# Five token tiles, one denominator matmul for two exp tiles, and four squares per norm matmul in an eight-core decoder step

## The chip, the cores and the metric

The kernel runs on all 8 cores of one Trainium2 chip, two dies of four cores, each core with its own share of the batch. The metric is the device time of the slowest core in microseconds (us). An execution comes in a fast state, or in a slow one in which the cores of one die are granted a lower TensorE clock (in the execution of 2127.61 us below, cores 0 to 3 had 0.811 to 0.821 and cores 4 to 7 0.991 to 0.993); all comparisons here are between fast executions. Ratios are computed as the mean time of one kernel's fast runs over the mean of the other's fast runs of the same rounds, so they are not quite the ratio of the medians that are quoted.

Engine names: PE is TensorE (PEld its weight loads), DVE VectorE, ACT ScalarE, POOL GpSimd, SP SyncE.

## The reference, cut to what matters

One layer of a decoder: half-step SwiGLU, a mixer, half-step SwiGLU, final norm. Per core: 2048 prompt tokens and 4 sample rows, width 1024. The mixer has dilated windowed attention (3 groups of 4 heads), a gated recurrence (HGRN2) and attention into 256 memory tokens.

```python
def rmsnorm(x, g):
    y = xf * lax.rsqrt(jnp.mean(xf * xf, axis=-1, keepdims=True) + EPS)   # four norms over D_MODEL
...
# attention group: 128-query blocks, each sees its own key block and the one before it ("back")
s = jnp.einsum('nbqhd,nbkhd->nbhqk', qb, kk) * (Dh ** -0.5)
lse = jax.nn.logsumexp(s, axis=-1); p = jnp.exp(s - lse[..., None])
o = jnp.einsum('nbhqk,nbkhd->nbqhd', p, vv)
...
# the groups are merged with weights proportional to their softmax denominators
# memory attention: softmax over 256 keys (two blocks of 128), 4 heads
```

## The kernel before

The program records operations with their dependencies. A list scheduler inside the kernel file then puts them in order with a fixed price for each operation and emits one in-order stream for each engine. The order on PE is frozen when the kernel is built, from prices. All operations are issued from the same helper, so the profile gives them all line 80, and groups are told apart by tile names: `br` is a ring of 13 bf16 tiles of 512 columns, `fr` a ring of 8 f32 tiles, `wp` weights, `hT` the normed input, `XA`/`XB` x and mixer scratch, `cb` constants (mask, ones), `ps`/`nd`/`hb` the PSUM banks.

```python
# the scheduler's prices (ns)
if eng == ACT:   p.cost = (155 if p.kind == "copy" else 260) + p.n * 0.833
elif eng == DVE: p.cost = 160 + p.n * (0.54 if p.bf else 1.04)
else:            p.cost = 230 + p.n * (0.9 if p.kind in ("tensor_copy", "memset") else 2.05)   # POOL
...
# squares: two chunks of x are squared, added on POOL, and go into one norm matmul
elif c % 2 == 0:
    s = pss[k, 0]; actf(s.t[:, 0:n], xv(k, c), AF.Square, ...)
else:
    actf(s2.t[:, 0:n], xv(k, c), AF.Square, ...)
    tt(POOL, b.t[:, 0:n], s.t[:, 0:n], s2.t[:, 0:n], ALU.add, ...)
    mm(p.t[:, 0:n], ones_n, b.t[:, 0:n], c == 1, c == 7, ...)
...
# q/k projection: four tiles of 512 tokens, then 16 matmuls of 4 columns for the sample rows
for ti, (t0, n) in enumerate(MTG):
    for c in range(8): mm(p.t[:, :], wv[:, a, c, :], hT[:, c, t0:t0 + n], c == 0, c == 7, ...)
...
# attention: exp of scores on ACT, causal mask as a product on DVE,
# then denominators (ones_b) and values block by block
actf(t.t[:, 0:o], p.t[:, 0:o], AF.Exp, [p.d], [t.d], scale=SCALE)
tt(DVE, tv, tv, mv, ALU.mult, [t.d, dm], [t.d])
...
for a in (1, 0):
    for q, (kb, po, oc, w) in enumerate(todo):
        lhs = ones_b if a else vb.t[:, kb, :]
        mm(p.t[:, oc:oc + w], lhs, t.t[:, o_ + po:o_ + po + w], ..., late=300.0)
...
# HGRN gates: three f32 sums of 128x512 per head and 512 tokens, on POOL
tt(POOL, t3.t[:, :], t3.t[:, :], t2.t[:, :], ALU.subtract, ...)
```

`late=300.0` asks the scheduler to place such a matmul 300 ns after its operands are ready by its prices, on top of a fixed 250 ns.

The softmax here doesn't subtract the row's maximum and nothing guards it: scores larger than these inputs give would overflow.

Of the kernel before, what the change touches and what calls it, by code (L numbers as in the profile page):

```python
# [174 lines left out]
class Prog:  # L175
# [7 lines left out]
    WAIT = 1200.0  # L183

# [58 lines left out]
    def schedule(self):  # L243
# [61 lines left out]
        while done < n:  # L305
# [76 lines left out]
            if e == ACT and o["aset"] not in (None, table):  # L382
                cost += self.TABLE
                table = o["aset"]
            o["t0"] = start
            if o["dma"]:
                issue = self.SWISSUE if e == POOL else 60.0
                end = free[e] = start + issue
                if o["pool"] == "bulk":
                    fin = start + 12000.0  # L390
                else:
                    pipe[e] = max(pipe[e], start + issue) + o["nbytes"] / self.DMA_RATE[e]
                    fin = pipe[e] + self.DMA_FIX
            else:
                end = free[e] = start + cost
                fin = end + (self.PEDRAIN if e == PE else 0.0)
# [30 lines left out]
    def emit(self):  # L427
# [50 lines left out]
        with ExitStack() as st:  # L478
# [6 lines left out]
            def run(name):  # L485
                def body(e):
                    b = Bound(e)
                    for o in order[name]:
                        for s, k in o["waits"]:
                            e.wait_ge(sems[s], semval[s][k])  # L490
# [20 lines left out]
MTG = [(0, 512), (512, 512), (1024, 512), (1536, 512)]  # L511
HALF = [(0, 1024), (1024, 1028)]
# [38 lines left out]
def build_nc():  # L551
# [153 lines left out]
    def sq(k, c, late=1000.0, pair=True):  # L705
# [4 lines left out]
        b = P.tile(brp)  # L710
        if not pair:
            actf(b.t[:, 0:n], xv(k, c), AF.Square, [dx[k][c]], [b.d])
            mm(p.t[:, 0:n], ones_n, b.t[:, 0:n], c == 0, c == 7, [b.d, dc], [p.d], late=late)
        elif c % 2 == 0:
# [3 lines left out]
        else:  # L718
            s, s2 = pss[k, 0], P.tile(frp)
            actf(s2.t[:, 0:n], xv(k, c), AF.Square, [dx[k][c]], [s2.d])  # L720
            tt(POOL, b.t[:, 0:n], s.t[:, 0:n], s2.t[:, 0:n], ALU.add, [s.d, s2.d], [b.d])
            mm(p.t[:, 0:n], ones_n, b.t[:, 0:n], c == 1, c == 7, [b.d, dc], [p.d], late=late)
# [171 lines left out]
    def att_proj(s, g, si):  # L894
# [5 lines left out]
        for a in range(2):  # L900
            dst = qk_r[si][a]
            for ti, (t0, n) in enumerate(MTG):
                p = P.tile(psM)
                for c in range(8):
                    mm(p.t[:, :], wv[:, a, c, :], hT[:, c, t0:t0 + n], c == 0, c == 7, [b.d] + hd(t0, n, c), [p.d])
                ov = dst.t.rearrange("p (r l) -> p r l", r=dil)[:, :, t0 // dil:(t0 + 512) // dil]
                iv = p.t[:, :].rearrange("p (l r) -> p r l", r=dil)
                dd = qk_d[si][a][ti]
                if a == 1 and (g == 2 or ti == 3):
                    f = P.tile(frp)  # L910
                    evac(f.t[:, :], p.t[:, :], [p.d], [f.d])
                    copy(POOL, ov, f.t[:, :].rearrange("p (l r) -> p r l", r=dil), [f.d], [dd])
                    m = min(512, win)
                    c0 = t0 if g == 2 else 0
                    P.dma(SP, lambda e, f=f, m=m, c0=c0: e.dma_start(out=pkt[g][s][:, c0:c0 + m], in_=f.t[:, 512 - m:512]), reads=[f.d])
                else:
                    evac(ov, iv, [p.d], [dd])
                yield 1
        p = P.tile(psM)
        for a in range(2):  # L920
            for c in range(8):
                mm(p.t[:, a * NS:(a + 1) * NS], wv[:, a, c, :], hT[:, c, T:NT], c == 0, c == 7, [b.d, dh[5][c]], [p.d])
        for a in range(2):
            copy(DVE, zs[:, a * 12 + g * 4 + s, :], p.t[:, a * NS:(a + 1) * NS], [p.d], [d_zs])
        copy(DVE, qsb[:, g * 4 + s, :], p.t[:, 0:NS], [p.d], [d_qsb])
# [6 lines left out]
    qk_d = [[[Dep() for _ in range(4)] for _ in range(2)] for _ in range(2)]  # L932

    def att_blocks(s, g, si):
# [5 lines left out]
        def dqk(a, lo, hi):  # L940
            if dil == 1:
                return [qk_d[si][a][x] for x in range(lo // 512, (hi - 1) // 512 + 1)]
            return qk_d[si][a]
        pts = {}

        def scores(kbs):
            p = P.tile(psM)
            o = 0
            lay = []
            for kb in kbs:  # L950
                w = 256 if (kb % nb) + 1 < nb else 128
                mm(p.t[:, o:o + w], kT[:, kb * 128:(kb + 1) * 128], qT[:, kb * 128:kb * 128 + w], True, True,
                   dqk(1, kb * 128, kb * 128 + 128) + dqk(0, kb * 128, kb * 128 + w), [p.d])
                lay.append((kb, o, w))
                o += w
            t = P.tile(brp)
            actf(t.t[:, 0:o], p.t[:, 0:o], AF.Exp, [p.d], [t.d], scale=SCALE)
            if len(lay) == 4:
                mv = mask2[:, 0:128].unsqueeze(1).to_broadcast([128, 4, 128])
                tv = t.t[:, 0:512].rearrange("p (a n) -> p a n", a=4)  # L960
                tt(DVE, tv, tv, mv, ALU.mult, [t.d, dm], [t.d])
            elif o == 512:
                mv = mask2.unsqueeze(1).to_broadcast([128, 2, 256])
                tv = t.t[:, 0:512].rearrange("p (a n) -> p a n", a=2)
                tt(DVE, tv, tv, mv, ALU.mult, [t.d, dm], [t.d])
            else:
                tt(DVE, t.t[:, 0:256], t.t[:, 0:256], mask2, ALU.mult, [t.d, dm], [t.d])
                tt(DVE, t.t[:, 256:384], t.t[:, 256:384], mask2[:, 0:128], ALU.mult, [t.d, dm], [t.d])
            for kb, o_, w in lay:
                pts[kb] = (t, o_, w)  # L970

        for m in range(4):
            todo = []
            if nb == 1:
                scores(range(4 * m, 4 * m + 4))
                for x in range(4):
                    todo.append((4 * m + x, 0, x * 128, 128))
            elif nb == 4:
                kbs = [r * 4 + m for r in range(4)]
                if m < 3:  # L980
                    scores(kbs[0:2])
                    scores(kbs[2:4])
                else:
                    scores(kbs)
                for r in range(4):
                    todo.append((kbs[r], 0, r * 128, 128))
                    if m > 0:
                        todo.append((kbs[r] - 1, 128, r * 128, 128))
            else:
                scores((4 * m, 4 * m + 1))  # L990
                scores((4 * m + 2, 4 * m + 3))
                for x in range(4):
                    todo.append((4 * m + x, 0, x * 128, 256 if x < 3 else 128))
                    if x == 0 and m > 0:
                        todo.append((4 * m - 1, 128, 0, 128))
# [4 lines left out]
            for a in (1, 0):  # L1000
                p = P.tile(psM)
                for q, (kb, po, oc, w) in enumerate(todo):
                    t, o_, _ = pts[kb]
                    lhs = ones_b if a else vb.t[:, kb, :]
                    mm(p.t[:, oc:oc + w], lhs, t.t[:, o_ + po:o_ + po + w], q == 0, True, [t.d, vb.d, dm], [p.d], chk=True, late=300.0)
# [252 lines left out]
    def mem_att(ti):  # L1258
# [3 lines left out]
        for hp in range(2):  # L1262
# [8 lines left out]
            for a in range(2):  # L1271
# [16 lines left out]
                for mc in range(2):  # L1288
                    mm(pd.t[:, :], ones_b, es[mc].t[:, :], mc == 0, mc == 1, [dm, es[mc].d], [pd.d])
# [179 lines left out]
    for _ in spread([A(), HG(), chain(*(mem_att(ti) for ti in range(3)))], [220, 105, 19]):  # L1469
        pass  # L1470
# [156 lines left out]
```

## Time and profile before

1804.74 us, median of three runs (1804.11 to 1805.31). The page of the slowest core starts with the span, then the busy time and share of each engine and its number of instructions:

```profile
span 1802.6 us, 33178 instructions; the slowest of 8 cores (1797.5 to 1802.6 us)
PE 1738.2 (96%) x12105; PEld 1109.0 (62%) x12171; DVE 674.7 (37%) x1391; ACT 730.4 (41%) x1266; POOL 405.2 (22%) x543
```

PE bounds the kernel. The two counts of PE differ: this core's trace lacks 66 matmul records. Cores 0, 1, 3, 5, 6 and 7 have all 12,171, and numbers below are means over cores with complete records, unless a core is named.

PE's busy share hides small waits, because the ends of matmuls are modelled: one of 512 columns is shown as 379 ns on average (core 3), though the next starts after 216. I therefore use the distance from each matmul's start to the next one's start. In an unbroken stream of bf16 its median on core 3 is 25 ns at 1 and at 4 columns, 56 at 128, 142 at 336 and 216 at 512. "PE work" below is the sum of estimated lengths, a line through these starts (columns/2.4 ns + 2.7, at least 25; for f32 I took four times the columns), and "idle" is what the distances hold beyond that.

| stage (us from start) | idle before, us |
|---|---|
| head, 0 to 70 (from the first matmul at about 10) | 23.8 |
| feed-forward, 70 to 480 | 0.1 |
| mixer, 480 to 1060 | 18.5 |
| merges and feed-forward, 1060 to 1700 | 1.6 |
| end, from 1700 to the last matmul | 5.4 |

The mixer, here on core 3: first the busy times of the engines in that window (columns: window, its length, then PE, PEld, DVE, ACT, POOL busy with counts, PE clock, DMA share, GB/s):

```profile
480.00:1060.00 580.00, 567.04 (x4136) 322.86 (x4135) 303.53 (x662) 354.10 (x611) 183.44 (x211) 1.00 0.61 129
```

Then who PE waited for there, as total, times and longest:

```profile
PE ps L80 <- DVE br L80: 2.4, 2, 1.8
PE hb L80 <- DVE XB L80: 1.7, 4, 0.6
...
PE nd L80 <- DVE br L80: 1.2, 2, 0.8
...
PE hb L80 <- DVE br L80: 0.4, 2, 0.3
```

And two groups of instructions of that window, by form: the HGRN sums on POOL, and the masks on DVE (`br<-br,cb`). The numbers after the bar are busy us and the mean ns of one:

```profile
L80 POOL TENSOR_TENSOR fr<-fr 128x512 f32<-128x512 f32 x48 | 64.4, 1353 | 40.5 <-ACT fr L80 20.5 <-DVE fr L80 19.9
L80 DVE TENSOR_TENSOR br<-br,cb 128x512 bf16<-128x512 bf16 x72 | 36.3, 514 | 30.8 <-ACT br L80 30.7
```

DVE is busy for about half of the mixer and POOL for a third. PE waits for `DVE br`, the masks, 4.0 us in all.

At the head, ACT's timeline (core 2) shows the exponential that finishes the first norm standing behind a square that waits for the second x tile:

```profile
14.17 0.56 ACT L80 ACTIVATE fr<-hb,vec 128x352 f32<-128x352 f32 x1 [0.69 <-PE hb L80]
21.17 0.57 ACT L80 ACTIVATE br<-XA,vec 128x336 bf16<-128x336 f32 x1 [6.44 <-DMA XA<-xt]
21.65 0.57 ACT L80 ACTIVATE fr<-fr,vec 128x352 f32<-128x352 f32 x1
```

### The profile page before, as it was taken

What the parts mean: (1) busy time and instruction counts of PE and PEld (TensorE: products, weight loads), DVE (VectorE), ACT (ScalarE), POOL (GpSimd) and SP (SyncE); (2) the same over time, 40 slices, a digit from 0 to 9 for tenths busy, and PEclk for the clock granted to TensorE, in tenths of its full rate; (3) what the DMA queues carried; (4) which work ended last, traced back from release to release, by engine and by line L of the source; (5) the groups of instructions that cost most, each with busy time, mean ns of one, the idle gap of its engine ahead of it and who ended that gap; (6) DMA issues with size and microseconds to landing.
All of it is one profiled execution on the core that took longest, in us unless ns stands there. A gap on an engine that the chain in (4) does not pass through costs nothing.

```text
span 1802.6 us, 33178 instructions; the slowest of 8 cores (1797.5 to 1802.6 us)
## 1 busy us (share of the span) xinstructions
PE 1738.2 (96%) x12105; PEld 1109.0 (62%) x12171; DVE 674.7 (37%) x1391; ACT 730.4 (41%) x1266; POOL 405.2 (22%) x543
## 2 busy tenths in 40 slices
PE   4999999999999999999999999999999999999996
PEld 1666666666655545555556566666666666666663
DVE  2223314222142435756576533543452221422213
ACT  5334414222145566758776633433342221322212
POOL 1112221001244051433431122322220002100021
PEclk9999999999999999999999999999999999999998
DMA  8486459656688554654547745596875447899562
GB/s 196 80 167 127 70 102 197 123 122 127 120 211 199 142 120 77 122 98 93 96 100 152 170 80 88 106 193 130 164 147 87 69 104 145 163 192 171 104 141 96
DMA packets 89391, 234.00 MB, mean 130 GB/s; under 512 B 32912, under 2 KB 40336, under 8 KB 86416
## 3 DMA queue, kind: packets, MB, share of 16 engines
q0 software_dynamic: 40608, 127.03, 44.6%
q1 hardware_dynamic: 46224, 59.26, 10.4%
q10 hardware_dynamic: 2400, 45.57, 8.7%
q8 instruction: 102, 1.67, 0.4%
q14 instruction: 57, 0.47, 0.1%
HBM read 321.27 MB, written 80.51 MB: 223 GB/s over the span
## 4 chain that ended last, share of the span: by engine, by line
PE 90%; DVE 3%; ACT 3%; issue 2%; DMA 1%; POOL 1%; DVEq 0%; ACTq 0%; SPq 0%; POOLq 0%
PE ps L80 49%; PE nd L80 33%; PE hb L80 8%; DVE XB L80 1%; ACT fr L80 1%; DMA XA<-xt 1%; DVE hT L80 1%; DVE br L80 1%; ACT br L80 0%; ACT L80 0%; ACT XA L80 0%; DVE fr L80 0%; POOL XA L80 0%; DVE XA L80 0%; POOL fr L80 0%
## 5 line engine op out<-in xcount | busy, mean ns | idle before, releaser
L80 PE MATMUL ps<-hT,wp 128*128 128x336 bf16 (+4 forms) x3839 | 637.2, 312 | 5.7 <-DVE hT L80 3.8
L80 PEld LDWEIGHTS ps<-hT,wp 128*128 128x128 bf16 x3856 | 365.6, 98 | 208.3 <-issue 6.4
L80 PE MATMUL nd<-hT,wp 128*128 128x336 bf16 (+4 forms) x2547 | 434.5, 312 | 1.4 <-ACT fr L80 0.2
L80 PEld LDWEIGHTS nd<-hT,wp 128*128 128x128 bf16 x2560 | 243.3, 98 | 134.7 <-issue 2.0
L80 ACT ACTIVATE fr<-ps,vec 128x336 f32<-128x336 f32 (+3 forms) x269 | 150.1, 560 | 343.8 <-PE ps L80 343.4
L80 PE MATMUL ps<-actb,wp 128*128 128x336 bf16 (+2 forms) x1612 | 253.8, 308 | 0.3 <-DVE XB L80 0.3
L80 PEld LDWEIGHTS ps<-actb,wp 128*128 128x128 bf16 x1612 | 157.3, 98 | 76.7 <-issue 0.6
L80 ACT ACTIVATE fr<-nd,vec 128x336 f32<-128x336 f32 (+3 forms) x185 | 103.4, 560 | 235.5 <-PE nd L80 235.2
L80 DVE TENSOR_TENSOR actb<-ps,fr 128x336 bf16<-128x336 f32 (+2 forms) x160 | 81.9, 514 | 266.2 <-PE ps L80 260.9
L80 PE MATMUL nd<-actb,wp 128*128 128x336 bf16 (+2 forms) x1076 | 173.0, 308 | 0.7 <-ACT fr L80 0.7
L80 POOL TENSOR_TENSOR fr<-fr 128x512 f32<-128x512 f32 (+3 forms) x96 | 108.0, 1132 | 161.0 <-DVE fr L80 140.2
L80 POOL DMA_DIRECT2D wp<-wgu x88 | 47.4, 538 | 400.3 <-PE ps L80 229.9
L80 PEld LDWEIGHTS nd<-actb,wp 128*128 128x128 bf16 x1076 | 105.0, 98 | 52.3 <-issue 1.0
L80 POOL TENSOR_TENSOR br<-fr 128x336 bf16<-128x336 f32 (+2 forms) x84 | 77.3, 923 | 181.2 <-ACT fr L80 181.0
L80 DVE TENSOR_TENSOR actb<-nd,fr 128x336 bf16<-128x336 f32 (+2 forms) x104 | 53.2, 513 | 173.2 <-PE nd L80 167.2
L80 ACT ACTIVATE fr<-XB,vec 128x352 f32<-128x352 f32 (+2 forms) x96 | 53.9, 577 | 138.5 <-DVE XB L80 138.5
L80 PE MATMUL hb<-hT,wp 128*128 128x512 bf16 (+1 forms) x514 | 95.2, 312 | 1.0 <-ACT fr L80 0.2
L80 ACT ACTIVATE fr<-XA,vec 128x336 f32<-128x336 f32 (+1 forms) x72 | 40.9, 578 | 130.2 <-DVE XA L80 130.2
L80 POOL DMA_DIRECT2D wp<-wd x64 | 34.8, 544 | 249.6 <-PE ps L80 128.5
L80 PE MATMUL hb<-br,cb 128*128 128x336 bf16 (+7 forms) x188 | 48.5, 300 | 28.9 <-ACT br L80 22.9
L80 ACT ACTIVATE fr<-fr,vec 128x512 f32<-128x512 f32 (+3 forms) x105 | 72.6, 700 | 5.0
L80 DVE SCALAR_TENSOR_TENSOR fr<-fr,ps 128x336 f32<-128x336 f32 (+2 forms) x85 | 43.2, 510 | 77.6 <-ACT fr L80 77.6
(244 smaller groups left out, 1630.9 us busy)
## 6 DMA issues: line engine op xcount, KB each, us to landing
wp<-wgu POOLq DMA_DIRECT2D x88, 512.0 KB, 8.9
wp<-wd POOLq DMA_DIRECT2D x64, 352.0 KB, 5.8
wp<-w_gb POOLq DMA_DIRECT2D x48, 384.0 KB, 8.8
wp<-w_hqf POOLq DMA_DIRECT2D x16, 512.0 KB, 8.3
vd<-br SPq DMA_DIRECT2D x48, 128.0 KB, 4.0
XA<-vd SPq DMA_DIRECT2D x12, 512.0 KB, 5.7
wp<-w_qk POOLq DMA_DIRECT2D x12, 512.0 KB, 7.6
pv<-fr SPq DMA_DIRECT2D x21, 256.0 KB, 6.4
```

The costliest lines, as they stand in the source:

```text
L80: return f(*[g(x) for x in a], **{n: g(x) for n, x in k.items()})
```

## The change

It takes work from PE in three places. The q/k projections run in five tiles that include the sample rows, so that the 4-column matmuls go. The exps of own and back blocks fill separate tiles, which are summed once, so that one 512-column matmul makes the denominator (in the memory attention the two exp tiles are summed too). Four squares instead of two are added before each norm matmul. The diff, cut to its core:

```diff
+QT = [(0, 416), (416, 416), (832, 416), (1248, 400), (1648, 404)]
 # norms
-        elif c % 2 == 0:
+        elif c % 4 == 0:
...
+            if c % 4 < 3:
+                tt(POOL, s.t[:, 0:n], s.t[:, 0:n], s2.t[:, 0:n], ALU.add, [s.d, s2.d], [s.d])
+                return
-            mm(p.t[:, 0:n], ones_n, b.t[:, 0:n], c == 1, c == 7, ...)
+            mm(p.t[:, 0:n], ones_n, b.t[:, 0:n], c == 3, c == 7, ...)
 # projections
-            for ti, (t0, n) in enumerate(MTG):
+            for ti, (t0, n) in enumerate(QT):
...
-        for a in range(2):
-            for c in range(8):
-                mm(p.t[:, a * NS:(a + 1) * NS], wv[:, a, c, :], hT[:, c, T:NT], ...)
 # attention
+            own = scores([(q, q) for q in qbs])
...
+                back = scores([(q - 1, q) for q in qbs[x0:]])
+                P.op((DVE, POOL), (lambda e, ...: e.tensor_tensor(out=ov, in0=i0, in1=i1, op=ALU.add),) * 2, reads=[own.d, back.d], writes=[sm.d])
+            dens = [(own, 0, x0)] * (0 < x0 < 4) + [(sm, x0 % 4, 4)]
-            for a in (1, 0):
+            for a in (0, 1):
 # memory attention
-                for mc in range(2):
-                    mm(pd.t[:, :], ones_b, es[mc].t[:, :], mc == 0, mc == 1, ...)
+                P.op((DVE, POOL), (... sm = es[0] + es[1] ...))
+                mm(pd.t[:, :], ones_b, sm.t[:, :], True, True, [dm, sm.d], [pd.d])
 # scheduler: DMA rates of the first 30 us (a hook for filler instructions is added, never switched on)
+                    pipe[e] = t + o["nbytes"] / (self.HEAD_RATE if t < self.HEAD else self.DMA_RATE[e])
 # interleave weights of the three streams of work in the mixer
-    for _ in spread([A(), HG(), ...], [220, 105, 19]):
+    for _ in spread([A(), HG(), ...], [236, 94, 22]):
```

More of the change, by code (lines that the diff above doesn't have):

```diff
@@ L183 @@
     WAIT = 1200.0
+    HEAD = 30000.0
+    HEAD_RATE = 150.0
+    fill, fill_end, FILL = None, 0.0, 65.0
     def __init__(self, nc, lanes=None):
@@ L384, in schedule @@
                 table = o["aset"]
+            if e == PE and order[PE] and self.fill is not None and start < self.fill_end:
+                o["fill"] = max(0, int((start - free[e] - 150.0) / self.FILL))
             o["t0"] = start
@@ L391, in schedule @@
                 else:
-                    pipe[e] = max(pipe[e], start + issue) + o["nbytes"] / self.DMA_RATE[e]
+                    t = max(pipe[e], start + issue)
+                    pipe[e] = t + o["nbytes"] / (self.HEAD_RATE if t < self.HEAD else self.DMA_RATE[e])
                     fin = pipe[e] + self.DMA_FIX
@@ L488, in body @@
                     for o in order[name]:
+                        for _ in range(o.get("fill", 0)):
+                            self.fill(e)
                         for s, k in o["waits"]:
@@ L709, in sq @@
         p = pss[k]
-        b = P.tile(brp)
         if not pair:
+            b = P.tile(brp)
             actf(b.t[:, 0:n], xv(k, c), AF.Square, [dx[k][c]], [b.d])
             mm(p.t[:, 0:n], ones_n, b.t[:, 0:n], c == 0, c == 7, [b.d, dc], [p.d], late=late)
-        elif c % 2 == 0:
+        elif c % 4 == 0:
             pss[k, 0] = P.tile(frp)
@@ L720, in sq @@
             actf(s2.t[:, 0:n], xv(k, c), AF.Square, [dx[k][c]], [s2.d])
+            if c % 4 < 3:
+                tt(POOL, s.t[:, 0:n], s.t[:, 0:n], s2.t[:, 0:n], ALU.add, [s.d, s2.d], [s.d])
+                return
+            b = P.tile(brp)
             tt(POOL, b.t[:, 0:n], s.t[:, 0:n], s2.t[:, 0:n], ALU.add, [s.d, s2.d], [b.d])
-            mm(p.t[:, 0:n], ones_n, b.t[:, 0:n], c == 1, c == 7, [b.d, dc], [p.d], late=late)
+            mm(p.t[:, 0:n], ones_n, b.t[:, 0:n], c == 3, c == 7, [b.d, dc], [p.d], late=late)
     def rstd(k):
@@ L901, in att_proj @@
             dst = qk_r[si][a]
-            for ti, (t0, n) in enumerate(MTG):
+            for ti, (t0, n) in enumerate(QT):
                 p = P.tile(psM)
                 for c in range(8):
-                    mm(p.t[:, :], wv[:, a, c, :], hT[:, c, t0:t0 + n], c == 0, c == 7, [b.d] + hd(t0, n, c), [p.d])
-                ov = dst.t.rearrange("p (r l) -> p r l", r=dil)[:, :, t0 // dil:(t0 + 512) // dil]
-                iv = p.t[:, :].rearrange("p (l r) -> p r l", r=dil)
+                    mm(p.t[:, 0:n], wv[:, a, c, :], hT[:, c, t0:t0 + n], c == 0, c == 7, [b.d] + hd(t0, n, c), [p.d])
+                np_ = min(n, T - t0)
+                ov = dst.t.rearrange("p (r l) -> p r l", r=dil)[:, :, t0 // dil:(t0 + np_) // dil]
@@ L908, in att_proj @@
                 dd = qk_d[si][a][ti]
-                if a == 1 and (g == 2 or ti == 3):
+                o = max(t0, T - win)
+                if a == 1 and o < t0 + np_:
                     f = P.tile(frp)
-                    evac(f.t[:, :], p.t[:, :], [p.d], [f.d])
-                    copy(POOL, ov, f.t[:, :].rearrange("p (l r) -> p r l", r=dil), [f.d], [dd])
-                    m = min(512, win)
-                    c0 = t0 if g == 2 else 0
-                    P.dma(SP, lambda e, f=f, m=m, c0=c0: e.dma_start(out=pkt[g][s][:, c0:c0 + m], in_=f.t[:, 512 - m:512]), reads=[f.d])
-                else:
-                    evac(ov, iv, [p.d], [dd])
@@ L918, in att_proj @@
-                yield 1
-        p = P.tile(psM)
-        for a in range(2):
-            for c in range(8):
-                mm(p.t[:, a * NS:(a + 1) * NS], wv[:, a, c, :], hT[:, c, T:NT], c == 0, c == 7, [b.d, dh[5][c]], [p.d])
-        for a in range(2):
-            copy(DVE, zs[:, a * 12 + g * 4 + s, :], p.t[:, a * NS:(a + 1) * NS], [p.d], [d_zs])
-        copy(DVE, qsb[:, g * 4 + s, :], p.t[:, 0:NS], [p.d], [d_qsb])
+                    evac(f.t[:, 0:n], p.t[:, 0:n], [p.d], [f.d])
+                    copy(POOL, ov, f.t[:, 0:np_].rearrange("p (l r) -> p r l", r=dil), [f.d], [dd])
@@ new lines, in att_proj @@
+                    dst_, src_ = pkt[g][s][:, o - (T - win):t0 + np_ - (T - win)], f.t[:, o - t0:np_]
+                    P.dma(SP, lambda e, dst_=dst_, src_=src_: e.dma_start(out=dst_, in_=src_), reads=[f.d])
+                else:
+                    evac(ov, p.t[:, 0:np_].rearrange("p (l r) -> p r l", r=dil), [p.d], [dd])
+                if np_ < n:
+                    copy(DVE, zs[:, a * 12 + g * 4 + s, :], p.t[:, np_:n], [p.d], [d_zs])
+                    if a == 0:
+                        copy(DVE, qsb[:, g * 4 + s, :], p.t[:, np_:n], [p.d], [d_qsb])
@@ L926, in att_proj @@
+                yield 0.82
         vbs[s, g] = vb
@@ L931, in build_nc @@
     vbs = {}
-    qk_d = [[[Dep() for _ in range(4)] for _ in range(2)] for _ in range(2)]
+    qk_d = [[[Dep() for _ in QT] for _ in range(2)] for _ in range(2)]
     def att_blocks(s, g, si):
@@ L941, in dqk, with scores @@
             if dil == 1:
-                return [qk_d[si][a][x] for x in range(lo // 512, (hi - 1) // 512 + 1)]
+                return [qk_d[si][a][x] for x, (t0, n) in enumerate(QT) if t0 < hi and lo < t0 + n]
             return qk_d[si][a]
-        pts = {}
-        def scores(kbs):
+        def scores(pairs):
             p = P.tile(psM)
-            o = 0
-            lay = []
-            for kb in kbs:
-                w = 256 if (kb % nb) + 1 < nb else 128
-                mm(p.t[:, o:o + w], kT[:, kb * 128:(kb + 1) * 128], qT[:, kb * 128:kb * 128 + w], True, True,
-                   dqk(1, kb * 128, kb * 128 + 128) + dqk(0, kb * 128, kb * 128 + w), [p.d])
-                lay.append((kb, o, w))
-                o += w
-            t = P.tile(brp)
-            actf(t.t[:, 0:o], p.t[:, 0:o], AF.Exp, [p.d], [t.d], scale=SCALE)
-            if len(lay) == 4:
-                mv = mask2[:, 0:128].unsqueeze(1).to_broadcast([128, 4, 128])
-                tv = t.t[:, 0:512].rearrange("p (a n) -> p a n", a=4)
-                tt(DVE, tv, tv, mv, ALU.mult, [t.d, dm], [t.d])
-            elif o == 512:
-                mv = mask2.unsqueeze(1).to_broadcast([128, 2, 256])
-                tv = t.t[:, 0:512].rearrange("p (a n) -> p a n", a=2)
-                tt(DVE, tv, tv, mv, ALU.mult, [t.d, dm], [t.d])
-            else:
-                tt(DVE, t.t[:, 0:256], t.t[:, 0:256], mask2, ALU.mult, [t.d, dm], [t.d])
-                tt(DVE, t.t[:, 256:384], t.t[:, 256:384], mask2[:, 0:128], ALU.mult, [t.d, dm], [t.d])
-            for kb, o_, w in lay:
-                pts[kb] = (t, o_, w)
@@ L972, in att_blocks @@
-        for m in range(4):
-            todo = []
-            if nb == 1:
-                scores(range(4 * m, 4 * m + 4))
-                for x in range(4):
-                    todo.append((4 * m + x, 0, x * 128, 128))
-            elif nb == 4:
-                kbs = [r * 4 + m for r in range(4)]
-                if m < 3:
-                    scores(kbs[0:2])
-                    scores(kbs[2:4])
-                else:
-                    scores(kbs)
-                for r in range(4):
-                    todo.append((kbs[r], 0, r * 128, 128))
-                    if m > 0:
-                        todo.append((kbs[r] - 1, 128, r * 128, 128))
-            else:
-                scores((4 * m, 4 * m + 1))
-                scores((4 * m + 2, 4 * m + 3))
-                for x in range(4):
-                    todo.append((4 * m + x, 0, x * 128, 256 if x < 3 else 128))
-                    if x == 0 and m > 0:
-                        todo.append((4 * m - 1, 128, 0, 128))
+            w = 128 * len(pairs)
@@ new lines, in scores @@
+            for x, (kb, qb) in enumerate(pairs):
+                mm(p.t[:, x * 128:x * 128 + 128], kT[:, kb * 128:(kb + 1) * 128], qT[:, qb * 128:(qb + 1) * 128], True, True,
+                   dqk(1, kb * 128, kb * 128 + 128) + dqk(0, qb * 128, qb * 128 + 128), [p.d])
+            t = P.tile(brp)
+            actf(t.t[:, 0:w], p.t[:, 0:w], AF.Exp, [p.d], [t.d], scale=SCALE)
+            back = pairs[0][0] != pairs[0][1]
+            mv = mask2[:, 128 * back:128 * back + 128].unsqueeze(1).to_broadcast([128, len(pairs), 128])
@@ new lines, in scores @@
+            tv = t.t[:, 0:w].rearrange("p (a n) -> p a n", a=len(pairs))
+            tt(DVE, tv, tv, mv, ALU.mult, [t.d, dm], [t.d])
+            return t
+        for m in range(4):
+            qbs = [r * 4 + m for r in range(4)] if nb == 4 else [4 * m + x for x in range(4)]
+            own = scores([(q, q) for q in qbs])
+            x0 = 0 if m and nb > 1 else 1 if nb == 16 else 4
+            todo = [(own, x, q, x) for x, q in enumerate(qbs)]
+            sm = own
+            if x0 < 4:
+                back = scores([(q - 1, q) for q in qbs[x0:]])
+                todo += [(back, x - x0, qbs[x] - 1, x) for x in range(x0, 4)]
+                sm = P.tile(brp)
+                ov, i0, i1 = sm.t[:, x0 * 128:512], own.t[:, x0 * 128:512], back.t[:, 0:(4 - x0) * 128]
+                P.op((DVE, POOL), (lambda e, ov=ov, i0=i0, i1=i1: e.tensor_tensor(out=ov, in0=i0, in1=i1, op=ALU.add),) * 2, reads=[own.d, back.d], writes=[sm.d])
+            dens = [(own, 0, x0)] * (0 < x0 < 4) + [(sm, x0 % 4, 4)]
@@ L999, in att_blocks @@
                 cells = d_acc[m]
-            for a in (1, 0):
+            for a in (0, 1):
                 p = P.tile(psM)
-                for q, (kb, po, oc, w) in enumerate(todo):
-                    t, o_, _ = pts[kb]
-                    lhs = ones_b if a else vb.t[:, kb, :]
-                    mm(p.t[:, oc:oc + w], lhs, t.t[:, o_ + po:o_ + po + w], q == 0, True, [t.d, vb.d, dm], [p.d], chk=True, late=300.0)
+                if a:
+                    for q, (t, lo, hi) in enumerate(dens):
+                        mm(p.t[:, lo * 128:hi * 128], ones_b, t.t[:, lo * 128:hi * 128], q == 0, True, [t.d, dm], [p.d], chk=True, late=300.0)
+                else:
+                    for q, (t, x, kb, qx) in enumerate(todo):
+                        mm(p.t[:, qx * 128:qx * 128 + 128], vb.t[:, kb, :], t.t[:, x * 128:x * 128 + 128], q == 0, True, [t.d, vb.d], [p.d], chk=True, late=300.0)
                 if nb == 1:
@@ L1287, in mem_att @@
                     mm(pv.t[:, :], mvb[:, mc, h * 128:(h + 1) * 128], es[mc].t[:, :], mc == 0, mc == 1, [d_mvb, es[mc].d], [pv.d])
-                for mc in range(2):
-                    mm(pd.t[:, :], ones_b, es[mc].t[:, :], mc == 0, mc == 1, [dm, es[mc].d], [pd.d])
+                sm = P.tile(brp)
+                P.op((DVE, POOL), (lambda e, sm=sm, es=es: e.tensor_tensor(out=sm.t[:, :], in0=es[0].t[:, :], in1=es[1].t[:, :], op=ALU.add),) * 2,
+                     reads=[es[0].d, es[1].d], writes=[sm.d])
+                mm(pd.t[:, :], ones_b, sm.t[:, :], True, True, [dm, sm.d], [pd.d])
                 r = P.tile(frp)
@@ L1467, in HG @@
         yield 2
-    for _ in spread([A(), HG(), chain(*(mem_att(ti) for ti in range(3)))], [220, 105, 19]):
+    for _ in spread([A(), HG(), chain(*(mem_att(ti) for ti in range(3)))], [236, 94, 22]):
         pass
```

## The prediction

> **What bounds it.** The page gives PE 96% busy over 1802.6 us, granted clock 0.993 on every core; the 50 us windows show PE at 50.0 of 50 in nearly all feed-forward stretches. From the starts of successive matmuls in the trace, one costs 25 ns at 4 columns, 56 at 128, 109 at 256, 142 at 336, 149 at 352, 216 at 512. [...] Priced so, all recorded matmuls are 1714 us. Idle beyond that: 10 us before the first matmul, 26 in the first 50 us, 33 between 500 and 1010 us (the mixer), 5.5 near 1784 us, 12 of tail. So PE work taken away is nearly all on the critical path.
>
> **Removed on PE** (estimates from those spacings):
> 1. Projections: per head and weight chunk 4x216+25 = 889 ns becomes 3x176+169+171 = 868. Times 192: -4.0 us. Columns and count are unchanged; only the 25 ns floor goes.
> 2. Denominators per head: dilation 1 falls from 31 blocks (1700 ns) to 866, dilation 4 from 28x56 = 1568 to 864, dilation 16 from 896 to 864. Splitting 256-column scores and values into 128 gives back 0.5 us in all. Net: -5.8 us.
> 3. Memory attention: 16 matmuls of 512 columns: -3.5 us.
> 4. Norms: 84 paired norm matmuls (56+36+16 by form, less 24 unpaired) become 42: -6.1 us.
> Together -19.3 us, 1.07%.
>
> **Added.** 44 sums on DVE (masks of that size take 510 ns) or POOL: some 22 us if all on DVE. 24 more, but shorter, evacuations (ACT 585, DVE 690 ns for 512 columns); 8 more K copies on POOL; 42 more f32 sums on POOL of 0.92 us. None bounds: in the busiest mixer windows DVE and ACT have 39 of 50 us, POOL 23. Exponentials stay. But the denominator now waits for exp, mask, exp, mask, sum instead of masked tiles alone, while its neighbours on in-order PE got shorter: I expect 2 to 6 us more small bubbles in the mixer. The tail's chain is no longer: one sum (0.9 us at 1788.7) follows the last square, as before.
>
> **Moved.** The order of all engines comes from the kernel's own scheduler, which now assumes other DMA rates for the first 30 us. In the timeline ACT put the second x tile's first square (waiting for its transfer until 21.2 us) before the first tile's exponential, so hT started at 22.3 us with PE idle from 14 to 22. An order that frees this may win 0 to 5 us; I count 2, since DMA is full until 31 us anyway. The filler hook is never switched on.
>
> **Sum.** 1804.7 - 19.3 + 4 - 2 - 1 (fewer waits where norms meet) = about 1786 us (1.0% faster). Range 1777 to 1796. Chances: faster by over 2% 0.05, within 2% 0.93, slower 0.02.
>
> **What would show it.** About 100 fewer matmuls; norm matmuls 66 instead of 108; no 4-column group left from the q/k projections; feed-forward stretches (1010 to 1780 us) shorter by 4 to 5 us, mixer by 9 to 13; the first gate matmul's time tells the head part.
>
> **What would make it wrong.** The scheduler reshuffles the mixer and its 33 us of idle change by more than 10; DVE's queue delays masks behind sums; the f32 ring (8 buffers), of which three now hold squares for four steps, stalls the silu stages; the head order gets worse.

1804.7 - 19.3 + 4 - 2 - 1 is 1785.4, the "about 1786 us". The terms for PE rest on the spacings listed; those at 400, 404 and 416 columns (169, 171 and 176 ns) were estimates from the listed ones, and after has 169, 170 and 176 (core 3). "DMA is full" is a mean DMA share of 0.91 to 1.04 from 10 to 31 us on core 2; it was 1.03 to 1.05 from there to 45 us, too.

## More of the kernel before

Idle includes waits and any matmul slowed by a lower clock. Two prices are too high, for all kernels alike: the eight f32 matmuls of 512 columns take 429 ns in the trace, where twice the columns would be priced at 429 and four times at 856, and 82 of the 128 matmuls of 64 rows and 128 columns (79 after) are 22 ns on average from the next start, where 56 are priced. Together they lower the mixer's idle by about 6 us before and after, so its level is a net figure and its changes are what counts.

PE work is 1728.1 us in 12,171 matmuls.

The mean of a mask is 514 ns, though the scheduler prices it at 436; the section on the result comes back to that.

## The result and the profile after

The median of four runs was 1849.81 us (1799.66 to 2127.61), but two of the four were slow. The three fast executions (a fifth run beside the four) took 1799.66, 1801.77 and 1803.05 us, the four of before 1804.11 to 1805.31. Executions in which one die ran at a lower clock are left out of the means. The ratio is 0.9982, interval 0.9962 to 1.0001: about 3 us won, if anything, where 19 were forecast. The page of the slowest core:

```profile
span 1798.1 us, 33399 instructions; the slowest of 8 cores (1790.8 to 1798.1 us)
PE 1729.8 (96%) x12069; PEld 1107.8 (62%) x12069; DVE 708.7 (39%) x1438; ACT 735.0 (41%) x1284; POOL 448.0 (25%) x594
```

There are 102 fewer matmuls (12,171 to 12,069), norm matmuls went from 108 to 66, and the 4-column matmuls on `hT` from 416 to 224. PE work fell from 1728.1 to 1708.7 us, by 19.4, as predicted. The idle did not stay:

| stage | idle before | after | change, us |
|---|---|---|---|
| head, 0 to 70 | 23.8 | 18.8 | -5.0 |
| feed-forward, 70 to 480 | 0.1 | 0.9 | +0.8 |
| mixer, 480 to 1060 | 18.5 | 34.9 | +16.4 |
| 1060 to 1700 | 1.6 | 3.4 | +1.8 |
| end | 5.4 | 6.2 | +0.8 |
| PE work | 1728.1 | 1708.7 | -19.4 |
| sum | | | -4.6 |

The sum agrees with the runs within their spread. The mixer, where 13.3 us of PE work were taken away (4.0 + 5.8 + 3.5, as priced in the prediction), gave 16.4 back. On core 3 the window has less PE work in the same time, and PE's clock is a little lower:

```profile
480.00:1060.00 580.00, 558.27 (x4057) 324.05 (x4056) 328.92 (x710) 361.22 (x632) 190.70 (x221) 0.99 0.60 127
```

PE's waits there, the largest first (before they were 2.4, 1.2 and 0.4 us for `DVE br`):

```profile
PE nd L80 <- DVE br L80: 5.2, 8, 1.7
PE ps L80 <- DVE br L80: 3.7, 7, 1.1
PE hb L80 <- DVE XB L80: 2.1, 4, 0.9
...
PE hb L80 <- DVE br L80: 0.7, 1, 0.7
```

Waits for masks and sums rose from 4.0 to 9.6 us. By starts of matmuls, the idle just ahead of value, denominator and norm matmuls (the readers of `br` with values or ones) rose from 6.5 to 16.5 us, 10.0 of the 16.4.

A second part is no wait. In the mixer of after, each complete core has two stretches of 3.4 us in which the granted clock is 0.50; before has none there. One of them on core 3 (the wait ahead of it, then its busy times in the columns of above):

```profile
506.75 0.41 PE L80 MATMUL nd<-wp,hT 128*128 128x512 bf16 x1 [1.88 <-DVE hT L80]
```

```profile
508.00:511.40 3.40, 3.40 (x12) 1.41 (x11) 2.17 (x6) 0.00 (x0) 3.12 (x1) 0.50 1.06 299
```

In it, matmuls of 512 columns start up to 427 ns apart and not 216. The two stretches hold 3.2 us of the idle (mean of the six complete cores), of which only 0.3 us is ahead of the readers named above. Both on core 3 follow a wait of about 2 us. What tips the clock was not tested: before has a wait of 1.9 us that no such stretch follows.

The groups of the same window, where `br<-br` are the new sums:

```profile
L80 POOL TENSOR_TENSOR fr<-fr 128x512 f32<-128x512 f32 x48 | 65.8, 1382 | 39.6 <-ACT fr L80 25.7 <-DVE fr L80 13.0 <-DVE zs L80 0.7
L80 DVE TENSOR_TENSOR br<-br,cb 128x512 bf16<-128x512 bf16 x72 | 42.6, 598 | 20.2 <-ACT br L80 19.9
L80 DVE TENSOR_TENSOR br<-br 128x512 bf16<-128x512 bf16 x39 | 22.2, 570 | 9.3 <-ACT br L80 7.1 <-DVE br L80 0.5
```

The same mask takes 598 ns on average now, and a sum 570. A mean hides what happens. On core 3, of 111 masks and sums of this form the 78 that overlap no POOL sum or copy take 420 ns on average, 426 at most. The 33 that overlap one take about 985 ns on average, up to 1758, and all 21 that took over 700 ns are among them. Before, 9 of 72 took over 700 ns, and 18 overlapped. The timeline shows such a place; lines are merged, so `x2` are two instructions in a row:

```profile
679.98 2.66 POOL L80 TENSOR_TENSOR fr<-fr 128x512 f32<-128x512 f32 x2 [0.17 <-DVE fr L80]
680.39 2.53 DVE L80 TENSOR_TENSOR br<-br,cb 128x512 bf16<-128x512 bf16 x2
...
681.66 0.38 PE L80 MATMUL nd<-br,XA 128*128 128x128 bf16 x4
...
683.07 0.38 PE L80 MATMUL nd<-br,XA 128*128 128x128 bf16 x4 [0.85 <-DVE br L80]
```

Two masks that should take 0.84 us take 2.53 us beside two POOL sums, and the value matmuls behind them wait 0.85 us.

Not every DVE instruction is slower there. Masks and sums have two SBUF operands. The 136 residual updates on DVE (`XA<-ps,XA` and its kin, one operand from PSUM) take 512 ns alone and 509 ns beside POOL, never over 526 (core 1). Why the two kinds differ the traces do not show.

The norm part shows the same. On core 1, the 112 products `hT<-XA/XB` that overlap no POOL sum or copy take 568 ns on average, 585 at most; the 32 that overlap one take 1001 ns, up to 2191. Near 1155 us, eight products `hT<-XA,vec,fr` (x and the reciprocal norm, both in SBUF) take 6.50 us beside POOL's sums of squares; a run of experiment e17 below has 3.92 us for the same eight:

```profile
1155.46 6.50 DVE L80 SCALAR_TENSOR_TENSOR hT<-XA,vec,fr 128x336 bf16<-128x336 f32 x8
1155.51 0.91 POOL L80 TENSOR_TENSOR br<-fr 128x336 bf16<-128x336 f32 x1
...
1156.37 0.90 POOL L80 TENSOR_TENSOR fr<-fr 128x336 f32<-128x336 f32 x1
...
1157.80 0.90 POOL L80 TENSOR_TENSOR fr<-fr 128x336 f32<-128x336 f32 x1
...
1162.52 0.73 PE L80 MATMUL ps<-hT,wp 128*128 128x336 bf16 x4 [0.98 <-DVE XA L80]
```

At the head, the exponential no longer stands behind the square (core 2, same lines as before):

```profile
14.39 0.55 ACT L80 ACTIVATE fr<-hb,vec 128x352 f32<-128x352 f32 x1 [0.69 <-PE hb L80]
15.04 0.59 ACT L80 ACTIVATE fr<-fr,vec 128x352 f32<-128x352 f32 x1
21.50 1.97 ACT L80 ACTIVATE br<-XA,vec 128x336 bf16<-128x336 f32 x4 [5.88 <-DMA XA<-xt]
```

One more reading helps with the experiments. The kernel's scheduler makes a plan from its own prices. It is no measurement, but it tells what the frozen order would do if every price were right, with the allowances before PE's readers counted in. The plan has 12.3 us of mixer idle before and 19.4 after. The chip has 18.5 and 34.9. So of the 16.4 us, about 7 are already in the new order, and the slip, what the chip adds to the plan, grew from 6.2 to 15.5 us; the stretches at half clock are 3.2 us of that.

### The profile page after: what moved, and what is told of

It is laid out like the page before. It is cut to its first block, busy times and chain, and to the rows that moved or that the text cites. A ratio compares the mean times of both kernels' runs of the same rounds, so it can differ in the third digit from the quotient of the medians.

```text
span 1798.1 us, 33399 instructions; the slowest of 8 cores (1790.8 to 1798.1 us)
## 1 busy us (share of the span) xinstructions
PE 1729.8 (96%) x12069; PEld 1107.8 (62%) x12069; DVE 708.7 (39%) x1438; ACT 735.0 (41%) x1284; POOL 448.0 (25%) x594
## 4 chain that ended last, share of the span: by engine, by line
PE 88%; DVE 5%; issue 2%; ACT 2%; DMA 2%; POOL 1%; DVEq 0%; ACTq 0%; SPq 0%; POOLq 0%
PE ps L80 48%; PE nd L80 32%; PE hb L80 7%; DMA XA<-xt 2%; DVE br L80 1%; DVE hT L80 1%; DVE XB L80 1%; ACT fr L80 1%; ACT br L80 1%; DVE XA L80 0%; DVE fr L80 0%; POOL fr L80 0%; ACT XA L80 0%; DVE actb L80 0%; ACT XB L80 0%
## 5 line engine op out<-in xcount | busy, mean ns | idle before, releaser
L80 PE MATMUL ps<-hT,wp 128*128 128x336 bf16 (+7 forms) x3960 | 656.4, 312 | 4.2 <-DVE XA L80 1.0
L80 PEld LDWEIGHTS ps<-hT,wp 128*128 128x128 bf16 x3960 | 377.7, 98 | 206.4 <-issue 6.5
L80 PE MATMUL nd<-hT,wp 128*128 128x336 bf16 (+7 forms) x2520 | 425.3, 312 | 0.5 <-DVE sob L80 0.5
L80 POOL TENSOR_TENSOR fr<-fr 128x352 f32<-128x352 f32 (+3 forms) x180 | 186.8, 1041 | 274.8 <-ACT fr L80 148.1
L80 PE MATMUL ps<-actb,wp 128*128 128x336 bf16 (+2 forms) x1598 | 249.2, 308 | 0.5 <-DVE XB L80 0.5
L80 ACT ACTIVATE fr<-XA,vec 128x336 f32<-128x336 f32 (+1 forms) x72 | 40.8, 577 | 131.4 <-DVE XA L80 131.2
L80 PE MATMUL hb<-hT,wp 128*128 128x416 bf16 (+4 forms) x464 | 90.0, 322 | 0.0
L80 PE MATMUL hb<-br,cb 128*128 128x336 bf16 (+5 forms) x100 | 34.0, 344 | 30.0 <-ACT br L80 22.6
L80 PEld LDWEIGHTS hb<-hT,wp 128*128 128x128 bf16 x464 | 39.5, 98 | 29.8 <-issue 1.0
```

The lines of the kernel that those rows point to most:

```text
L80: return f(*[g(x) for x in a], **{n: g(x) for n, x in k.items()})
```

## The experiments

The theories:

- **Lock**: two-operand DVE instructions (masks, new sums, norm products) are held up by POOL instructions (420 against 985 ns above; what does it in the chip was not shown, "lock" is only a name). The scheduler knows nothing of it, and in-order PE waits.
- **Chain**: the longer path exp, mask, exp, mask, sum is itself what starves PE.
- **Load**: DVE and ACT are too full in the mixer.
- **Luck**: before was a lucky order, or after an unlucky one.

Times are of fast executions; the idle is from the profiled one.

### e1: HGRN sums from POOL to DVE, in after

```diff
-            tt(POOL, t3.t[:, :], t3.t[:, :], t2.t[:, :], ALU.subtract, ...)
-            tt(POOL, t1.t[:, :], t3.t[:, :], t1.t[:, :], ALU.subtract, ...)
-            tt(POOL, t2.t[:, :], t3.t[:, :], t2.t[:, :], ALU.add, ...)
+            the same three with DVE
```

> After, with the 48 f32 sums and differences of the HGRN gates (128x512, 1.38 us each on POOL) moved to DVE; nothing else. Lock theory (a DVE product or sum of two SBUF operands is held up by a POOL instruction that runs at the same time: 0.42 us alone, 1.06 us mean where they overlap): the mean of masks and own+back sums falls from 0.60 and 0.57 to under 0.48 us, PE's idle in the mixer (480 to 1060 us) falls from 35 to 22-27 us, and the kernel takes 1789-1793 us. Chain theory (the longer path exp, mask, exp, mask, sum by itself starves in-order PE) and load theory (DVE, ACT too full): DVE gets 33 us more work, so the idle stays at 35 or grows, 1800-1810 us.

(On core 3 the 28 masks and sums of after that overlap a POOL sum by 0.1 us or more take 1.06 us on average; with shorter overlaps and copies it is the 985 ns above.)

Four runs, 1792.15 to 1794.28 us, ratio to before 0.9931. Mixer idle is 27.5 us, from 34.9. The groups on core 3, then PE's longest wait and those for `DVE br`:

```profile
L80 DVE TENSOR_TENSOR br<-br,cb 128x512 bf16<-128x512 bf16 x72 | 32.8, 466 | 11.5 <-ACT br L80 11.2
L80 DVE TENSOR_TENSOR br<-br 128x512 bf16<-128x512 bf16 x37 | 16.0, 434 | 8.5 <-ACT br L80 7.0
```

```profile
PE ps L80 <- ACT br L80: 4.0, 4, 2.0
...
PE nd L80 <- DVE br L80: 1.7, 1, 1.7
PE hb L80 <- DVE br L80: 1.4, 2, 0.9
...
PE ps L80 <- DVE br L80: 0.8, 3, 0.3
```

DVE does more work in the mixer (344.9 us against 328.9 on core 3), and still the masks are quicker and the kernel gains 8 us. The idle ahead of values, denominators and norms falls from 16.5 to 6.7 us, what it was before the change. That speaks for the lock and against load on DVE. The idle and the times came out at or a little above the upper edges of what I expected, since other idle in the mixer rose by 2.5 us: waits for exps (`ACT br`) went from 1.4 us in after to 5.2, and stretches at half clock hold 3.5 us.

### e2: the same move in before

The diff is that of e1.

> Control of e1 on the kernel before. Lock theory: fewer masks there and no sums, so less to win: mixer idle from 18.5 to 14-16 us, 1800-1803 us. Load theory: 1805-1812 us.

Four runs, 1800.62 to 1803.67 us, ratio 0.9974; mixer idle 14.4 us. As the lock theory had it: there was less to win before the change, 4 us against 7.4. (There are as many masks of 512 columns before, 72, contrary to what I wrote; what is missing are the sums.)

### e3: more room before the readers, in after

```diff
-  ..., [p.d], chk=True, late=300.0)      # value and denominator matmuls
+  ..., [p.d], chk=True, late=1200.0)
```

> After, with the scheduler's allowance before value and denominator matmuls raised from 300 to 1200 ns, so that PE has other matmuls placed ahead of them. Lock theory: delays of up to about 1.1 us are now covered; waits of PE on masks and sums fall from 16 us to under 6, mixer idle 35 to 22-26, kernel 1790-1794 us, though masks stay at 0.6 us. Load theory (throughput of DVE and ACT is short): waits move elsewhere, idle stays near 35.

Fast runs 1791.82 to 1794.04 us (one of four was slow), ratio 0.9926; mixer idle 27.4 us. The masks and sums are still held up (531 and 617 ns on core 3), but PE hardly waits for them:

```profile
PE nd L80 <- ACT br L80: 2.8, 3, 2.2
PE hb L80 <- ACT br L80: 2.1, 2, 1.1
...
PE ps L80 <- DVE br L80: 0.9, 2, 0.6
...
PE nd L80 <- DVE br L80: 0.3, 1, 0.3
```

The time is won without taking the delay away, by not letting PE stand behind it. Load as the main cause is refuted a second time, since no engine got less work. The remaining idle is again larger than I expected (22 to 26): stretches at half clock hold 5.1 us of it, and exps are now what PE waits for longest.

### e4: no sum, two denominator matmuls, in after

```diff
-                P.op((DVE, POOL), (... sm = own + back ...))
-            dens = [(own, 0, x0)] * (0 < x0 < 4) + [(sm, x0 % 4, 4)]
+            dens = [(own, 0, 4, 0)] + ([(back, 0, 4 - x0, x0)] if x0 < 4 else [])
```

> After, without the sum of own and back tiles in the attention: the denominator takes two matmuls (own, back) instead of one, at about 6 us more of PE work; 28 DVE sums fewer. Lock theory: masks still collide, waits on sums go: mixer idle 35 to 28-31, so the time is about the same, 1800-1804. Chain theory: the sum was the link too many, idle falls to 20-24, 1795-1798.

1806.85 us; mixer idle 32.2. The chain theory's 20 to 24 us is refuted: without the sum in the path most of the idle stays. Idle and time are also a little above what the lock theory gave. Masks are still at 0.57 us. But the idle just ahead of values, denominators and norms fell from 16.5 to 10.1 us while other idle rose, 1.6 us of it in stretches at half clock. So the sum has a share in the waits, through the longer path or because it is itself held up; this run doesn't separate the two.

### e5: both cures, in after

```diff
 HGRN sums on DVE as in e1, late=1000.0 (e3 had 1200.0), and
-            P.op(eng, lambda e: e.tensor_copy(...), reads=reads, writes=writes)
+            P.op(eng, lambda e: e.tensor_copy(...), reads=reads, writes=writes, slow=1.4 if eng == POOL else 1.0)
-    for _ in spread([A(), HG(), ...], [236, 94, 22]):
+    for _ in spread([A(), HG(), ...], [252, 104, 24]):
```

> After, with the HGRN sums on DVE as in e1, the allowance at 1000 ns as in e3, POOL copies priced 1.4 times as high in the scheduler (measured 0.9 us for 400 columns, priced at 0.59), interleave weights 252, 104, 24. The plan that the kernel's own scheduler makes has 15.4 us of idle in the mixer. Lock theory: with collisions fewer and covered the chip comes close to the plan: mixer idle 19-24 us, 1785-1790 us. If e1 and e3 cure the same waits and the rest has other causes: 26-28 us, about 1792.

Fast runs 1783.81 to 1784.17 us, ratio 0.9880. Mixer idle is 18.7 us against a plan of 15.4, so the slip is down to 3.3 us, all a little better than expected. Stretches at half clock hold 1.0 us, from 3.2. The idle ahead of values, denominators and norms is 3.0 us. This run mixes several edits, so it shows that the slip can be cured, not what each edit is worth; part of the gain (4 us) is the better plan.

### e6: more room, in before

The diff is that of e3.

> Control of e3: before with the allowance at 1200 ns. Planned mixer idle 15.2 us instead of 12.3. Lock theory: the waits on masks (5.6 us) go, so the measured mixer idle is 16-18 us against 18.5, 1802-1805 us. If the larger allowance were just good for any order, it would win 7 us here too: idle 11-12.

1808.96 us; mixer idle 22.2. This is a miss of both expectations: waits on masks vanished from the top of PE's list, but the new order has 2.9 us more planned idle and other waits came in. A larger allowance is thus no general gain. It paid in after, where the slip was large.

### e7: the attention sums alone, in before

```diff
 before, with only the attention hunk of the change (own and back tiles, sum, one denominator matmul)
```

> Before plus only the attention part of the change (own and back tiles, one sum, one denominator matmul). PE work 5.8 us less; planned mixer idle 15.7 us. Lock theory: most of the slip comes with this part: mixer idle 25-30 us instead of 18.5, 1806-1811 us, no gain or a loss. If the slip comes from the five tiles or the rest: idle about 22, 1802-1803 us.

Fast runs 1802.69 to 1804.44 us, ratio 0.9989, interval 0.9972 to 1.0005. PE work is 5.8 us less and mixer idle 23.0 us: 4.5 of the 5.8 given back. My expectation for the lock theory (25 to 30) was wrong. The sums alone do not bring most of the slip.

### e8: the norms alone, in before

```diff
 before, with only the hunk in sq()
```

> Before plus only the four squares per norm matmul. PE work 6.1 us less; the longer chain on POOL shows as 1-3 us of waits in the feed-forward stages (1130 to 1400 us) and at the tail: 1799-1802 us; mixer idle 18-19 as before.

Fast runs 1801.47 to 1801.96 us, ratio 0.9978. The mixer is unchanged (18.1 us). The stages 70 to 300, 1130 to 1200 and 1200 to 1400 us together rose from 2.4 to 5.9 us and the end from 5.4 to 6.2: 4.3 of the 6.1 us given back, where I had expected 1 to 3.

### e9 to e12: null changes

```diff
-    SEM = 90.0
+    SEM = 84.0        # e9 after, e11 before; 94.0 in e10 after, e12 before
```

> Null change of after: the scheduler's price of a semaphore is 84 ns instead of 90, which reorders some 900 matmuls but changes no instruction. Planned mixer idle 18.8 us (19.4 in after). Rival 'unlucky order': measured mixer idle scatters by 6 us or more around the kernel's typical value, and falls to 24-29 us here. Lock theory, systematic: 32-37 us, 1799-1804 us.

> As e9 with 94 ns (planned idle 20.2 us). Unlucky order: below 30. Systematic: 33-38 us, 1800-1805 us.

> Null change of before, 84 ns; planned mixer idle 12.3 us as in before. If before was a lucky order: 23-28 us. If systematic: 17-20 us, 1803-1806 us.

> As e11 with 94 ns (planned idle 11.7 us). Lucky order: 23-28. Systematic: 17-20 us, 1802-1806 us.

| | mixer idle, us | one look, us |
|---|---|---|
| after, e9, e10 | 34.9, 40.8, 34.8 | 1807.24, 1806.61 |
| before, e11, e12 | 18.5, 19.0, 19.7 | 1809.26, 1811.30 |

These runs reorder hundreds of instructions and change none. The two kernels' idle does not overlap, so luck is refuted as the main cause: the extra idle belongs to the change, though a null change alone can move it by 6 us. e9's idle (32 to 37 expected) and the times of all four were above my ranges. Weight loads outside the mixer have a part in that: e12's slowest core waited 3.3 us for one transfer of `w_gb`, e10's core 2 waited 6.1 us. Only the slowest core's time counts, so single times are worse evidence here than the idle of a stage.

### e13 to e16: the other parts

```diff
 e13: before, with only the five tiles
 e14: before, with only the sum in the memory attention
 e15: after, with the attention of before (no own/back tiles, no sum there)
 e16: before, with only the scheduler's DMA rates for the first 30 us
```

> Before plus only the q/k projections in five tiles. PE work 4.0 us less, planned mixer idle 16.8 us (12.3 in before). If the parts act each by the plan plus the same slip as before (6 us): mixer idle 22-24 us, 1804-1807 us. If the five tiles are what brings the slip: 28 us or more, over 1809.

> Before plus only the sum in the memory attention. PE work 3.5 us less, planned mixer idle 18.1 us. By plan plus 6 us of slip: 23-26 us, 1806-1810 us. If that part brings the slip: 29 or more.

> After without the own and back tiles and their sum (attention as before). Planned mixer idle 16.5 us. If the attention sums act only together with the rest: slip as before, mixer idle 22-25 us, PE work 5.8 us more than after, 1797-1800 us. If five tiles or memory sum bring the slip without them: 28-34 us, 1803-1808.

> Before plus only the scheduler's other DMA rates for the first 30 us. Mixer as before (18-19 us idle). If they are what won the head: idle in the first 70 us falls from 24 to 18-20, 1798-1801 us. If it was the rest of the change: 1804-1805.

| part | PE work, us | planned mixer idle | mixer idle | one look, us |
|---|---|---|---|---|
| none (before) | | 12.3 | 18.5 | |
| attention sums (e7) | -5.8 | 15.7 | 23.0 | see e7 |
| five tiles (e13) | -4.0 | 16.8 | 21.7 | 1807.09 |
| memory sum (e14) | -3.5 | 18.1 | 25.3 | 1816.87 |
| all but attention sums (e15) | -13.6 | 16.5 | 28.2 | 1802.87 |
| all (after) | -19.4 | 19.4 | 34.9 | see result |
| DMA rates (e16) | 0 | 12.3 | 18.1 | 1798.79 |

No single part is to blame. Each of the three mixer parts brings idle: 4.5, 3.2 and 6.8 us, 14.5 of the 16.4. But of these 14.5 us, 13.7 (3.4, 4.5 and 5.8) are in the plans of those runs already; no part alone makes the slip grow by more than 1.1 us, where all together add 9.3. So the slip comes with the combination, or with the interleave weights: the runs with a slip above 10 us (after, e9, e10, e15) all have after's weights 236, 94, 22, and no part was run alone with them. The change without its new weights is a rival that was not tested. The memory sum gives back more than it takes away. Its time of 1816.87 us includes something else: core 3, the slowest, waited 4.4 us for a weight transfer at the merge. In e15, five tiles and memory sum without the attention sums bring 28.2 us, at the lower edge of the second alternative and above the first. The DMA rates alone cut the head's idle from 23.8 to 18.2 us, so the 5 us at the head are theirs. Their one look, 1798.79 us, is also as fast as the whole change (before took 1806.40 in the same round): what after won, the rates win alone.

### e17: sums of squares on DVE, on top of e5

```diff
-                tt(POOL, s.t[:, 0:n], s.t[:, 0:n], s2.t[:, 0:n], ALU.add, [s.d, s2.d], [s.d])
-            tt(POOL, b.t[:, 0:n], s.t[:, 0:n], s2.t[:, 0:n], ALU.add, [s.d, s2.d], [b.d])
+            the same two with DVE
```

> e5 with the f32 sums of squares moved from POOL to DVE (126 of them, about 0.5 us each there instead of 0.9). Lock theory for the norms: the products hT<-XA/XB fall from a mean of 0.66 us to about 0.57, PE's idle in the stages 70-300, 1130-1200 and 1200-1400 us falls from 5.7 us together to under 3, and the idle near the end from 6.2 to about 4; 1778-1782 us. If the norms' idle comes from the longer chain itself: no change there, 1783-1787 us.

Fast runs 1774.88 to 1776.38 us, ratio 0.9832 (0.9813 to 0.9852). The products that were held up near 1155 us run unhindered (DVE's timeline, core 1):

```profile
1136.71 3.92 DVE L80 SCALAR_TENSOR_TENSOR hT<-XA,vec,fr 128x336 bf16<-128x336 f32 x8 [0.21 <-ACT fr L80]
```

All 144 products `hT<-XA/XB` take 568 ns on average, 585 at most (core 1). In after they take 664, 17 of them over 750 and one 2191 ns; before the change it was 601, 7 over 750. Idle in the three feed-forward stages fell from 5.7 to 1.3 us, at the end from 6.2 to 2.1 us, of which 2.4 come back after the last matmul (14.7 us to the end of the span, from 12.3). Time and idle are better than expected. That fits the norm part, too, giving its time back where its products run beside POOL's sums. It doesn't rule out the longer chain: the chain has the same links here, but a sum takes 0.51 us on DVE where it took 0.92 on POOL.

### e18: the cures without the change

```diff
 before, with the DMA rates of e16, HGRN sums on DVE, POOL copies priced 1.4 times,
-    for _ in spread([A(), HG(), ...], [220, 105, 19]):
+    for _ in spread([A(), HG(), ...], [228, 108, 24]):
```

> Before with the scheduler's new DMA rates, HGRN sums on DVE, POOL copies priced 1.4 times, weights 228, 108, 24 (best of 247 plans; planned mixer idle 9.2 us), but none of the change's three parts. If the cures and rates alone make e5's time: about 1785. If the change's 19 us of PE work are really won in e5: 1794-1798 us here, with mixer idle of 11-14.

Two fast runs, 1797.01 and 1797.03 us (three others were slow). Mixer idle 15.3 us, a little over what I expected. Against this kernel, e5 is 13 us faster (1797.0 to 1784.0, over two sessions) and e17 21 us (1775.8), with 19.4 us less PE work. Neither is a pure price of the change: `late` stays at 300 here, nearly all of the 3.2 us won in the mixer is the better plan (9.2 us against 12.3; the slip is 6.1 us, against 6.2), and before with its own sums of squares on DVE was not run, though e17's moved sums also shorten the end.

## Why the prediction was wrong, point by point

- **What bounds the kernel, and the work removed**: right. 19.4 us of PE work went against 19.3 forecast, 102 matmuls against "about 100", 66 norm matmuls as said.
- **The idle of the mixer before**: "33 between 500 and 1010 us" was too large. I took it from core 2, whose trace lacks 66 matmul records, and a missing matmul looks like idle. Cores with all records have 18.5 us.
- **The step that failed**: "None bounds: ... I expect 2 to 6 us more small bubbles in the mixer." It was 16.4 us. I judged DVE and POOL by busy shares, and priced the sums from a mean duration as if each engine ran alone. What counted here was whether one instruction was late when in-order PE reached its reader (9.6 us of waits for `DVE br` on core 3). A mask or sum on DVE that takes 0.42 us alone took about 1.0 us where it met a POOL instruction. Of the 16.4 us, 10.0 lie directly ahead of value, denominator and norm matmuls. They went to the level of before when the POOL sums were moved (e1) and a little below it when room was left (e3, 5.7 us). Another 3.2 us are matmuls at half clock, which the prediction didn't have at all.
- **"DVE's queue delays masks behind sums"**, under what would make it wrong, named the right engine and the wrong reason: masks are delayed by POOL (985 ns beside it against 420), not only by the queue, and the five tiles and the memory sum bring idle too. The first item of that list, mixer idle that changes by more than 10 us, came true.
- **"1 (fewer waits where norms meet)"**: wrong in sign. The norm part brought 3.4 us of idle in the feed-forward stages and the end, most likely, as I read e8 and e17, because its products take 1001 ns beside POOL's sums and 568 alone.
- **"The tail's chain is no longer"**: the chain is as said, but the idle at the end rose by 0.8 us. The extra POOL sum runs beside the final products on DVE. I saw that in the timeline and tested it only together with the rest, in e17.
- **The head**: mechanism right, size off. 5.0 us were won against 2 counted, and e16 shows that the DMA rates did it.
- **The sum**: 19.4 + 5.0 won, 16.4 + 3.4 given back, so 4.6 us by the idle and about 3 by the runs.

What stays open: about 7 of the mixer's 16.4 us are in the scheduler's plan already, and whether the rest needs the new interleave weights was not tested. That shorter PE work leaves the same chains on ACT and DVE less to hide behind is argued, not shown; e5 only shows that another plan of the same change has 4 us less. Also open is why the memory sum brings more idle than the attention sums, which are more numerous; 5.8 of its 6.8 us are planned.

## What to carry to other kernels

When PE work is taken away by adding elementwise sums, ask how long the new instructions take beside what other engines run at that time, not how busy the engines are. Here tensor-tensor instructions on DVE with both operands in SBUF took 420 ns alone and 985 beside POOL instructions, among them sums of 1.4 us, and in-order PE reads their results: moving the POOL work (e1) took 7.4 us off the mixer's idle, more room for the reader (e3) 7.5. Before pricing a change by idle time, check that the trace has all records (two cores of eight lacked 66 of 12,171 matmuls before, and the mixer's idle read 32.6 us there and not 18.5), and compare the idle of each stage, since a tuned order gives removed work back where nobody looks. Look at the granted clock of each stage too: here 3.2 us of the idle were matmuls at half clock.
